# Turning the written key and the normed outputs through DRAM and VectorE's 32x32 blocks in a one-core decoder layer

## The chip, the cores and the metric

The kernel runs on one core of a Trainium2 chip. The metric is the device time of one launch in microseconds (us). The engines are named as in the profile: PE (TensorE), with PEld for its weight loads, DVE (VectorE), ACT (ScalarE), POOL (GpSimd) and SP (SyncE, which here only issues DMAs).

## The reference

One decoder layer over 512 tokens of width 2048, in float32. RWKV time mixing on 16 heads of 64 channels runs beside a multi-scale pooling group, and both are gated and go through one output projection:

```
h = rms_norm(x, norm_g);  z = h @ w_in          # r, k, v, two loras | gate | pool input | pool gate
r, k, v, wd, ad = token_shift_lerp(z)
S_t = S_{t-1} (diag(w_t) - kk_t^T (a_t * kk_t)) + v_t^T k_t ;  y_t = S_t r_t     # per head, 512 steps
y   = head_group_norm(y) * ln_w + ln_b ;  y_rwkv = (y + bonus) * silu(gate)
y_pool = (window means - token) @ w_pool * pool_scale * silu(gate)
x = x + concat(y_rwkv, y_pool) @ w_out
x = x + sigmoid(x @ w_pg + b_pg) * (p @ w_ple) ;  out = rms_norm(x, final_g)
```

## The kernel before, in words

Channels lie on the 128 partitions and tokens along the free dimension. The 16 heads are worked as 8 head pairs j = 0..7 of 128 channels, and the 512 tokens as 8 chunks `ch` of 64. Each float32 projection is three 128x512 matmuls on a high and a low half (`mm3`). A weight chunk of 512 rows x 128 columns is loaded by SP (`raw`, L129), its high half cast by ACT (`whi`, L132), its low half formed by DVE (`wlo`, L133). Each of the three has four buffers, so a load waits for the `wlo` four chunks back, and a cast waits until PE has used the chunk four back; a chunk is 12 matmuls.

PE's program order is written out by hand. `pump(n)` puts n of the large projection matmuls (`zb`, `zg`, `zr`, `zk`, `zv`, ...) between the small ones of the recurrence as filler. A scheduler places the instructions of the other engines when the kernel is built; DVE, ACT and SP then run them strictly in that order. For each pair, `recur(j)` runs the chunks of pair j while pair j+1 is got ready:

- `prepare(j+1)`: the decayed query `ar` and the written key `bk` (two DVE instructions, L596 and L600), and the bonus halves `kph`, `kpl` (L138).
- `scores(j+1)`, after chunk 0: 32 matmuls `pm<-ar,bk`, the masked matrices `mt` (L623), the bonus sum `pbo` and `bv`; four 32-row stores `nd` (L639) and two loads `n` (`n32`, L644) bring blocks of `mt` back in another arrangement. SP issues all of them, in one queue with the weight loads.
- `invert(j+1)`: 31 steps of two small DVE instructions, `tm` (L657) and `xw` (L661), spread over chunks 2 to 7, then `xd` (L665) and `x<-xd` (L672) through DRAM.
- in each chunk: `py` -> `zs` (DVE, L784) -> `pu` -> `uv` (ACT, L794) -> `ps<-uv,bkn` -> `sbd` (DVE, L804 and L806). At ch 3 and ch 7 a visit of 8 small matmul pairs `py<-uv,mt` completes four chunks of outputs, and ACT copies them to `ysb` (L827).
- behind chunk 7: `bn_stats`, `bn_aggr` and a short chain of 128x8 instructions, then eight instructions that normalise `ysb` (L851).
- `gather(j+1)`: TensorE transposes of v (`pv`) and of `bk` (`pbk`, eight of 128x128, copied to `bkn` by ACT, L700); `pending` runs the `finish` of the pair before (`pyt`, four TensorE transposes of `ysb`; ACT L860, DVE L861 and L862, store `yd`). Then two DVE transposes `y<-x` (L723), one for each half of the partitions, whose results `pq` reads with both halves alternating; `scale_key` (the reciprocal of L572); `pq`, `pmv`, `px`. `gather(j)` also computes what pair j+1 needs from k (`prepare_key`, `norm_key`, `scale_key`).

After the last pair come the output projection (`acc_o`, from `yin` read back from `yd`, split into `yhi` and `ylo`) and the embedding gate (`acc_g`).

Of the kernel before, what the change touches and what calls it, by code (L numbers as in the profile page):

```python
# [34 lines left out]
def trunk_kernel(ctx: ExitStack, tc: tile.TileContext, x, p, norm_g, w_in, mu, w0, w_up, a0, a_up,  # L35
# [84 lines left out]
    def dp(o, i):  # L120
        return dprm[:, o + i:o + i + 1]
# [34 lines left out]
    def mm(*a, **k):  # L156
        i = nc.tensor.matmul(*a, **k)  # L157
        return tc.keep_in_program_order(i) if pin[0] else i

    def tr(*a):  # L160
        i = nc.tensor.transpose(*a)
        return tc.keep_in_program_order(i) if pin[0] else i
# [414 lines left out]
    def prepare(j):  # L577
        k_, r_, v_ = need("k", j), need("r", j), need("v", j)
        pw, ipw, tha = pws.pop(j)
        kk = kks.pop(j)  # L580
        if j + 1 < NJ:
            load_ab(j + 1)


        ar = rw.tile([P, NCH // 2, 4, C], F32, name=f"ar{j}", tag="ar", bufs=2)
        bk = rw.tile([P, NCH // 2, 4, C], F32, name=f"bk{j}", tag="bk")
        k4 = kk.rearrange("p (q c t) -> p q c t", c=2, t=C)
        pw4 = pw.rearrange("p (q c) t -> p q c t", c=2)
# [7 lines left out]
        nc.vector.tensor_tensor(bk[:, :, 0::3, :], kp.rearrange("p (q c t) -> p q c t", c=2, t=C), i4, ALU.mult)  # L596
# [3 lines left out]
        nc.vector.tensor_tensor(bk[:, :, 1:3, :], k4, i4, ALU.mult)  # L600
        nc.vector.scalar_tensor_tensor(kp, r_, dp(49, j), kp, ALU.mult, ALU.mult)
        kph = rw.tile([P, T], F32R, name=f"kph{j}", tag="t", bufs=4)
        kpl = rw.tile([P, T], F32R, name=f"kpl{j}", tag="t", bufs=4)
        split(kph, kpl, kp)

        st_[j] = dict(pw=pw, ar=ar, bk=bk, v_=v_, kp=(kph, kpl))

    def scores(j):
        ar, bk, v_ = (st_[j][n_] for n_ in ("ar", "bk", "v_"))
        kph, kpl = st_[j].pop("kp")  # L610

        mt = rw.tile([P, 2, 8, 2, C], F32, name=f"mt{j}", tag="mt", bufs=2)
        pm = [[psM.tile([P, T], F32, name=f"pm{j}_{par}0", tag="m"),
               psY.tile([P, T], F32, name=f"pm{j}_{par}1", tag="y")] for par in range(2)]
        for par in range(2):
            for q in range(4):
                for h in range(2):
                    rows = slice(64 * h, 64 * h + 64)
                    mm(pm[par][h][:, q * P:(q + 1) * P], bk[rows, q, 2 * par:2 * par + 2, :],
                       ar[rows, q, 2 * par:2 * par + 2, :], start=True, stop=True)  # L620
        for par in range(2):
            for h in range(2):
                nc.vector.tensor_tensor(mt[:, par, h::2, :, :],  # L623
                                        pm[par][h].rearrange("p (u a t) -> p u a t", u=4, a=2),
                                        msk[:, par:par + 2, :].unsqueeze(1).to_broadcast([P, 4, 2, C]), ALU.mult)


        ps = psM.tile([P, T], F32, name=f"pbo{j}", tag="m")
        mm(ps, blk, kph, start=True, stop=False)
        mm(ps, blk, kpl, start=False, stop=True)  # L630
        bv = rw.tile([P, T], F32, name=f"bv{j}", tag="bv", bufs=2)
        nc.vector.tensor_tensor(bv, ps, v_, ALU.mult)

        nd = dram.tile([2, 2, 8, 32, 32], F32, name=f"nd{j}", tag="nd")
        for par in range(2):
            pb = 64 * (1 - par)
            for b in range(2):
                rows = slice(pb + 32 * b, pb + 32 * b + 32)
                nc.sync.dma_start(out=nd[par, b].rearrange("u r c -> r u c"),  # L639
                                  in_=mt[rows, par, :, 1 - par, 32 * b:32 * b + 32])  # L640
        nb = []
        for i in range(2):
            t_ = rw.tile([P, 16, 32], F32, name=f"n32{j}_{i}", tag=("kk", "kp")[i])
            nc.sync.dma_start(out=t_, in_=nd[:, :, :, 16 * i:16 * i + 16, :].rearrange(  # L644
                "a b u r c -> (a b u) r c").unsqueeze(0).to_broadcast([4, 32, 16, 32]))
            nb.append(t_)
        st_[j].update(mt=mt, nb=nb, bv=bv)


    def invert(j):  # L650
# [26 lines left out]

    def gather(j):
        d = st_[j]
        bk, v_, mt = d.pop("bk"), d.pop("v_"), d["mt"]  # L680
        if j + 1 < NJ:
            prepare_key(j + 1)
            decay_and_rate(j + 1)
# [7 lines left out]
        nc.scalar.copy(uv[64:128, 1::2, :], pv[64:128])  # L691


        bkn = rw.tile([P, NCH, P], F32, name=f"bkn{j}", tag="bkn")
        for hf in range(2):
            ps = psM.tile([P, T], F32, name=f"pbk{j}_{hf}", tag="m")
            for i in range(4):
                ch = 4 * hf + i
                tr(ps[:, i * P:(i + 1) * P], bk[:, ch // 2, 2 * (ch % 2):2 * (ch % 2) + 2, :], ident)
            nc.scalar.copy(bkn[:, 4 * hf:4 * hf + 4, :], ps.rearrange("p (c n) -> p c n", n=P))  # L700

        pump(H4)

        d.update(uv=uv, bkn=bkn)
        if j + 1 < NJ:
            norm_key(j + 1)
        pump(H5)
        if pending:
            pending.pop()()
        pump(HX)  # L710

        x1 = d["x1"]
# [34 lines left out]
        nc.scalar.copy(zsp[0][64:128, :].rearrange("p (h t) -> p h t", h=2), psv[64:128, 0:2, :])  # L747
        nc.scalar.copy(mv.rearrange("p q (h t) -> p (q h) t", h=2), psv)
        d["mv"] = mv
        pump(2 * H1)  # L750


    def recur(j, work, between):
        d = st_.pop(j)
        pw, ar, mt, bv, uv, bkn, mv, x1 = (d[n_] for n_ in ("pw", "ar", "mt", "bv", "uv", "bkn", "mv", "x1"))
        hop = [0]
        HC1, HC2, HC3 = HC
        lead = [None]
# [8 lines left out]


        ysb = rw.tile([P, NT, P], F32, name=f"ysb{j}", tag="t", bufs=4)
        py = None  # L770
        for ch in range(NCH):
            par, q = ch % 2, ch // 2
            pb = 64 * (1 - par)
# [1 line left out]
            pcc = pw[:, ch, C:C + 1]  # L775
            sl = slice((ch % 4) * P, (ch % 4 + 1) * P)
            if ch % 4 == 0:
                py = psY.tile([P, T], F32, name=f"py{j}_{ch}", tag="y")
            zs = zsp[par]
            if ch > 0:  # L780
                mm(py[:, sl], ar[:, q, 2 * par:2 * par + 2, :], cur, start=ch in (1, 4), stop=True,
# [15 lines left out]
            if ch < NCH - 1:  # L797
# [12 lines left out]
                if ch < NCH - 2:  # L810
                    for h in range(2):
                        hc = slice(64 * h, 64 * h + 64)
                        nc.gpsimd.tensor_scalar(s0p[hc, :], nxt[hc, hc], pcn[hc], None, ALU.mult)  # L813
            if ch % 4 == 3:
                for qq in range(2):
                    for h in range(2):
                        for pr in range(2):
                            c_ = ch - 3 + 2 * qq + pr
                            yr = slice(64 * pr, 64 * pr + 64)
                            o_ = (2 * qq + pr) * P + 64 * h  # L820
                            mm(py[yr, o_:o_ + 64], mt[:, pr, 2 * (c_ // 2) + h, pr, :],
                                             uv[:, c_, 64 * h:64 * h + 64], start=False, stop=True,
                                             skip_group_check=True)
                py4 = py.rearrange("p (s c) -> p s c", c=P)
                for pr in range(2):
                    yr = slice(64 * pr, 64 * pr + 64)
                    nc.scalar.copy(ysb[yr, q - 1:q + 1, :], py4[yr, pr::2, :])  # L827
# [22 lines left out]
        for i in range(8):  # L850
            nc.vector.tensor_scalar(y8[:, i, :], y8[:, i, :], mvr[:, i, 0:1], rs8[:, i, :],  # L851
                                    ALU.subtract, ALU.mult)

        def finish():
            sg = need("g", j)
            ps = psM.tile([P, T], F32, name=f"pyt{j}", tag="m")
# [28 lines left out]
    for j in range(NJ):  # L885
# [292 lines left out]
```

## Time and profile before

| quantity | value |
|---|---|
| time, median of 3 runs | 1094.34 us (1093.44 to 1331.12) |
| profiled execution | 1094.06 us |
| its span, first to last instruction | 1092.3 us |
| granted TensorE clock, mean | 0.998 |
| PE / PEld / DVE / ACT / POOL busy | 1067.4 / 879.1 / 707.9 / 448.2 / 74.4 us |
| DMA packets | 178485, 138.56 MB |

The span is what the trace covers; the profiled execution's own time is 1.8 us more. The head pairs take from about 38 to 711 us, about 75 us each, and the output projection and gate the rest. Busy times are sums; since DVE, ACT and SP run in a fixed order, what an instruction has ahead of it on its engine matters as much as what it reads.

### The profile page before, as it was taken

What the parts mean: (1) busy time and instruction counts of PE and PEld (TensorE: products, weight loads), DVE (VectorE), ACT (ScalarE), POOL (GpSimd) and SP (SyncE); (2) the same over time, 40 slices, a digit from 0 to 9 for tenths busy, and PEclk for the clock granted to TensorE, in tenths of its full rate; (3) what the DMA queues carried; (4) which work ended last, traced back from release to release, by engine and by line L of the source; (5) the groups of instructions that cost most, each with busy time, mean ns of one, the idle gap of its engine ahead of it and who ended that gap; (6) DMA issues with size and microseconds to landing.
All of it is one profiled execution on the core that took longest, in us unless ns stands there. A gap on an engine that the chain in (4) does not pass through costs nothing.

```text
span 1092.3 us, 17194 instructions
## 1 busy us (share of the span) xinstructions
PE 1067.4 (98%) x6060; PEld 879.1 (80%) x6060; DVE 707.9 (65%) x1835; ACT 448.2 (41%) x917; POOL 74.4 (7%) x180
## 2 busy tenths in 40 slices
PE   5999999999999999999999999999999999999996
PEld 4888878888888888787888788888888888888885
DVE  6687867878779679678886956454433424445366
ACT  7633534435335335353443344544222222233337
POOL 2100010110110110100101101000000000000000
PEclk9999999999999999999999999999999999999999
DMA  7433433332423333333334242774534438454534
GB/s 233 116 97 97 112 92 79 102 101 72 127 81 102 105 91 89 95 83 90 94 93 120 79 138 94 231 242 163 171 123 141 164 97 261 129 187 147 174 105 154
DMA packets 178485, 138.56 MB, mean 127 GB/s; under 512 B 34677, under 2 KB 139742, under 8 KB 178398
## 3 DMA queue, kind: packets, MB, share of 16 engines
q1 hardware_dynamic: 157694, 103.89, 32.2%
q10 hardware_dynamic: 20704, 33.56, 9.5%
q8 instruction: 48, 0.79, 0.3%
q14 instruction: 39, 0.32, 0.1%
HBM read 118.02 MB, written 18.87 MB: 125 GB/s over the span
## 4 chain that ended last, share of the span: by engine, by line
PE 88%; DVE 5%; DMA 3%; ACT 2%; issue 1%; SPq 0%; ACTq 0%; DVEq 0%
PE acc_o L157 16%; PE acc_g L157 16%; PE zb L157 15%; PE zv L157 8%; PE zr L157 7%; PE zg L157 7%; PE zk L157 6%; DMA n<-nd 2%; PE py L157 2%; PE pple L157 2%; PE pu L157 2%; PE pm L157 1%; PE pp L157 1%; PE ps L157 1%; PE pmv L157 1%
## 5 line engine op out<-in xcount | busy, mean ns | idle before, releaser
L133 DVE TENSOR_TENSOR wlo_g<-raw_g,whi_g 128x512 fp32r<-128x512 f32 x84 | 56.9, 683 | 78.7 <-ACT whi_g L132 78.5
L157 PE MATMUL zb<-hhi,whi_b 128*128 128x512 f32 x256 | 106.3, 415 | 0.0
L133 DVE TENSOR_TENSOR wlo_o<-raw_o,whi_o 128x512 fp32r<-128x512 f32 x64 | 43.9, 690 | 92.3 <-ACT whi_o L132 92.2
L157 PE MATMUL zb<-hhi,wlo_b 128*128 128x512 f32 x256 | 100.5, 393 | 0.0
L157 PE MATMUL acc_o<-whi_o,ylo 128*128 128x512 f32 x256 | 100.2, 391 | 0.0
L157 PE MATMUL acc_o<-whi_o,yhi 128*128 128x512 f32 x256 | 99.9, 390 | 0.0
L157 PE MATMUL zb<-hlo,whi_b 128*128 128x512 f32 x256 | 99.8, 390 | 0.0
L157 PE MATMUL acc_o<-wlo_o,yhi 128*128 128x512 f32 x256 | 99.7, 389 | 0.0
L132 ACT CAST whi_g<-raw_g 128x512 fp32r<-128x512 f32 x84 | 51.9, 620 | 105.5 <-PE acc_g L157 60.3
L157 PE MATMUL acc_g<-whi_g,x2hi 128*128 128x512 f32 x208 | 81.2, 391 | 0.0
L157 PE MATMUL acc_g<-wlo_g,x2hi 128*128 128x512 f32 x208 | 81.0, 389 | 0.0
L157 PE MATMUL acc_g<-whi_g,x2lo 128*128 128x512 f32 x208 | 80.6, 389 | 0.0
L132 ACT CAST whi_o<-raw_o 128x512 fp32r<-128x512 f32 x64 | 39.9, 623 | 97.8 <-PE acc_o L157 97.8
L813 POOL TENSOR_SCALAR s0p<-sbd,pw 64x64 f32<-64x64 f32 x96 | 56.7, 590 | 338.5 <-DVE sbd L806 253.7
L132 ACT CAST whi_b<-raw_b 128x512 fp32r<-128x512 f32 x64 | 39.7, 620 | 87.1 <-PE zv L157 34.9
L133 DVE TENSOR_TENSOR wlo_b<-raw_b,whi_b 128x512 fp32r<-128x512 f32 x64 | 43.7, 684 | 34.2 <-ACT whi_b L132 33.0
L157 PEld LDWEIGHTS zb<-hhi,wlo_b 128*128 128x128 f32 x256 | 48.0, 188 | 11.0
L661 DVE TENSOR_TENSOR xw<-xw,tm 128x60 f32<-128x60 f32 (+24 forms) x248 | 51.9, 209 | 6.8
L157 PEld LDWEIGHTS acc_o<-wlo_o,yhi 128*128 128x128 f32 x256 | 48.1, 188 | 10.0
L157 PEld LDWEIGHTS acc_o<-whi_o,ylo 128*128 128x128 f32 x256 | 48.1, 188 | 9.9
L157 PEld LDWEIGHTS acc_o<-whi_o,yhi 128*128 128x128 f32 x256 | 48.1, 188 | 9.6
L157 PEld LDWEIGHTS zb<-hhi,whi_b 128*128 128x128 f32 x256 | 48.3, 189 | 8.4
(285 smaller groups left out, 2546.8 us busy)
## 6 DMA issues: line engine op xcount, KB each, us to landing
raw_b<-in_w_in_dram SPq DMA_DIRECT2D x64, 256.0 KB
raw_o<-in_w_out_dram SPq DMA_DIRECT2D x64, 256.0 KB
raw_g<-in_w_pg_dram SPq DMA_DIRECT2D x64, 256.0 KB
raw_k<-in_w_in_dram SPq DMA_DIRECT2D x32, 256.0 KB
raw_r<-in_w_in_dram SPq DMA_DIRECT2D x32, 256.0 KB
raw_v<-in_w_in_dram SPq DMA_DIRECT2D x32, 256.0 KB
raw_g<-in_w_in_dram SPq DMA_DIRECT2D x32, 256.0 KB
n<-nd SPq DMA_DIRECT2D x16, 256.0 KB
```

The source lines that it names most:

```text
L132: nc.scalar.copy(hi, raw)
L133: nc.vector.tensor_tensor(lo, raw, hi.bitcast(F32), ALU.subtract)
L157: i = nc.tensor.matmul(*a, **k)
L661: nc.vector.tensor_tensor(xw[:, 0:n_, s + 1:32], xw[:, 0:n_, s + 1:32], tm[:, 0:n_, 0:w_], ALU.add)
L813: nc.gpsimd.tensor_scalar(s0p[hc, :], nxt[hc, hc], pcn[hc], None, ALU.mult)
```

## The change

The transposes of the written key and of the normed outputs leave TensorE. `bk` is stored to DRAM (`bkd`, SP) as soon as it is made; in `scores` four SP loads bring it back as `bg`, with 32x32 blocks arranged so that DVE's transpose, which turns each 32x32 block in its place, finishes the job: `turn_key` is one 128x512 DVE instruction for each half, `bkn<-bg`. The normalised `ysb` goes the same way: store `yb`, four loads `yg` (`fetch`, in the first half of the old `finish`), one DVE transpose `yo<-yg` and the rest as before (`finish`, moved behind half of the last pump of `gather`). `bg` and `yg` share the buffer tag of `bk` (one buffer). `bkn` becomes one tile for all pairs. The `py<-uv,mt` products of all eight chunks, and the copies to `ysb`, come in one visit at ch 7 instead of two.

```diff
 def prepare(j):
-        st_[j] = dict(pw=pw, ar=ar, bk=bk, v_=v_, kp=(kph, kpl))
+        bkd = dram.tile([P, NCH * P], F32, name=f"bkd{j}", tag="bkd")
+        nc.sync.dma_start(out=bkd, in_=bk.rearrange("p q s c -> p (q s c)"))
+        st_[j] = dict(pw=pw, ar=ar, bk=bk, bkd=bkd, v_=v_, kp=(kph, kpl))
+    bkn = rw.tile([P, NCH, P], F32, name="bkn")
+    def turn_key(j, hf):
+        cs = slice(4 * hf, 4 * hf + 4)
+        nc.vector.transpose(bkn[:, cs, :].rearrange("p c (b k) -> p (c b) k", k=32),
+                            st_[j]["bg"][:, cs, :, :].rearrange("p c b k -> p (c b) k"))
 def scores(j):
+        bg = rw.tile([P, NCH, 4, 32], F32, name=f"bg{j}", tag="bk")
+        for q in range(4):
+            nc.sync.dma_start(out=bg[32 * q:32 * q + 32],
+                              in_=st_[j]["bkd"].rearrange("(b k) (c q i) -> q k c b i", b=4, q=4, i=32)[q])
 def gather(j):
-        bkn = rw.tile([P, NCH, P], F32, name=f"bkn{j}", tag="bkn")
-        for hf in range(2):
-            ps = psM.tile([P, T], F32, name=f"pbk{j}_{hf}", tag="m")
-            for i in range(4):
...
-            nc.scalar.copy(bkn[:, 4 * hf:4 * hf + 4, :], ps.rearrange("p (c n) -> p c n", n=P))
+        if j == 0:
+            turn_key(0, 0)
+            turn_key(0, 1)
         pump(H4)
...
         if pending:
-            pending.pop()()
+            pending[0][0]()
         pump(HX)
...
-        pump(2 * H1)
+        pump(H1)
+        if pending:
+            pending.pop()[1]()
+        pump(H1)
 def recur(j, work, between):
+            if ch in (4, 7) and j + 1 < NJ:
+                with tc.issue_after(lead[0].ins):
+                    turn_key(j + 1, ch // 7)
-            if ch % 4 == 3:
...
+            if ch == NCH - 1:
+                for c0 in range(0, NCH, 4):
...
+        yb = dram.tile([P, T], F32, name=f"yb{j}", tag="yb")
+        nc.sync.dma_start(out=yb, in_=ysb.rearrange("p t c -> p (t c)"))
+        def fetch():
+            yg = rw.tile([P, NCH, 4, 32], F32, name=f"yg{j}", tag="bk")
+            for q in range(4):
+                nc.sync.dma_start(out=yg[32 * q:32 * q + 32, 0:NT],
+                                  in_=yb.rearrange("(b k) (t q i) -> q k t b i", b=4, q=4, i=32)[q])
+            fetched.append(yg)
         def finish():
-            for tt in range(NT):
-                tr(ps[:, tt * P:(tt + 1) * P], ysb[:, tt, :], ident)
...
-            nc.scalar.activation(yo, ps, AF.Identity, scale=dp(57, j), bias=dp(65, j))
+            nc.vector.transpose(yo.rearrange("p (b k) -> p b k", k=32), yg[:, 0:NT].rearrange("p t b k -> p (t b) k"))
+            nc.scalar.activation(yo, yo, AF.Identity, scale=dp(57, j), bias=dp(65, j))
...
-    pump(HE)
-    pending.pop()()
+    pump(HE // 2)
+    pending[0][0]()
+    pump(HE // 2)
+    pending.pop()[1]()
```

The scheduler also arranges the instructions of DVE and SP differently around the new ones. Three places follow; the digit behind a name's stem is the pair or chunk set it belongs to (`bk4` is pair 4's, `wlo_k5_2` is piece 2 of pair 5's k weights), the digits behind the last underscore only number the buffer, and line numbers are those of each kernel's own file.

SP's queue around pair 4's loads `n`, during `recur(3)`, before:

```order
L129 DMA raw_r5_2_2634<-in_w_in_dram 128x4x128
L639 DMA nd4_4661<-mt4_4631 32x8x32 x4
L129 DMA raw_r5_3_2669<-in_w_in_dram 128x4x128
L644 DMA n324_0_4666<-nd4_4661 128x1x512
L644 DMA n324_1_4668<-nd4_4661 128x1x512
L129 DMA raw_v5_0_2675<-in_w_in_dram 128x4x128
L129 DMA raw_v5_1_2732<-in_w_in_dram 128x4x128
```

and with the change:

```order
L607 DMA bkd4_4561<-bk4_4546 128x1024
L648 DMA nd4_4657<-mt4_4627 32x8x32 x2
L658 DMA bg4_4666<-bkd4_4561 32x32x32
L648 DMA nd4_4657<-mt4_4627 32x8x32
L129 DMA raw_r5_3_2667<-in_w_in_dram 128x4x128
L648 DMA nd4_4657<-mt4_4627 32x8x32
L658 DMA bg4_4666<-bkd4_4561 32x32x32
L129 DMA raw_v5_0_2673<-in_w_in_dram 128x4x128
L129 DMA raw_v5_1_2735<-in_w_in_dram 128x4x128
L653 DMA n324_0_4662<-nd4_4657 128x1x512
L653 DMA n324_1_4664<-nd4_4657 128x1x512
```

The two loads `n` have moved behind two weight loads and two of the `bg` loads.

DVE's order ahead of pair 4's `mt`, that is, what runs up to and around PE's `pm` of `scores(4)`, before (`bk4` L596 is seven rows further up):

```order
L600 TENSOR_TENSOR bk4_4552<-kk4_4294,ipw4_4314 128x4x128
L133 TENSOR_TENSOR wlo_k5_0_2461<-raw_k5_0_2458,whi_k5_0_2460 128x512
L601 SCALAR_TENSOR_TENSOR kp4_4553<-sr4_4076,dprm_133,kp4_4553 128x512
L804 TENSOR_SCALAR sbd1_567<-ps3_0_4594,pw3_3343 64x64 x2
L526 TENSOR_TENSOR as5_4550<-ar5_4547,as5_4550 64x128
L138 TENSOR_TENSOR kpl4_4564<-kp4_4553,kph4_4563 128x512
L133 TENSOR_TENSOR wlo_k5_1_2489<-raw_k5_1_2486,whi_k5_1_2488 128x512
L133 TENSOR_TENSOR wlo_k5_2_2495<-raw_k5_2_2492,whi_k5_2_2494 128x512
L623 TENSOR_TENSOR mt4_4631<-pm4_00_4632,msk_108 128x4x128
```

and with the change:

```order
L819 TENSOR_SCALAR sbd1_567<-ps3_0_4590,pw3_3350 64x64 x2
L133 TENSOR_TENSOR wlo_k5_1_2479<-raw_k5_1_2476,whi_k5_1_2478 128x512
L133 TENSOR_TENSOR wlo_k5_2_2485<-raw_k5_2_2482,whi_k5_2_2484 128x512
L883 STREAM_TRANSPOSE yo2_4525<-yg2_4386 128x512
L596 TENSOR_TENSOR bk4_4546<-kp4_4547,ipw4_4320 128x4x2x64
L600 TENSOR_TENSOR bk4_4546<-kk4_4300,ipw4_4320 128x4x128
L885 TENSOR_TENSOR yo2_4525<-yo2_4525,bv2_2719 128x512
L601 SCALAR_TENSOR_TENSOR kp4_4547<-sr4_4069,dprm_133,kp4_4547 128x512
L886 TENSOR_TENSOR yo2_4525<-yo2_4525,sg2_2829 128x512
L138 TENSOR_TENSOR kpl4_4558<-kp4_4547,kph4_4557 128x512
L632 TENSOR_TENSOR mt4_4627<-pm4_00_4628,msk_108 128x4x128
```

Both halves of `bk4` now stand behind `yo2<-yg2`, whose buffer they take over, and behind `wlo_k5_2`.

DVE's order around the two transposes `y<-x` of `gather(1)` (`y11`), before:

```order
L851 TENSOR_SCALAR ysb0_1663<-ysb0_1663,mvr0_2327,rs80_2344 128x64 x5
L133 TENSOR_TENSOR wlo_b1_2_1385<-raw_b1_2_1382,whi_b1_2_1384 128x512
L851 TENSOR_SCALAR ysb0_1663<-ysb0_1663,mvr0_2327,rs80_2344 128x64 x3
L568 TENSOR_SCALAR kk2_2367<-pss2_2438 128x512
L723 STREAM_TRANSPOSE y11_2507<-x11_2258 32x256 x2
L572 RECIPROCAL kk2_2367<-kk2_2367 128x512
```

and with the change:

```order
L568 TENSOR_SCALAR kk2_2375<-pss2_2433 128x512
L150 TENSOR_TENSOR nt80_2353<-nt80_2353,rs80_2350 128x8
L731 STREAM_TRANSPOSE y11_2497<-x11_2253 32x256
L151 SCALAR_TENSOR_TENSOR rs80_2350<-nt80_2353,rs80_2350 128x8
L572 RECIPROCAL kk2_2375<-kk2_2375 128x512
L133 TENSOR_TENSOR wlo_b1_3_1411<-raw_b1_3_1408,whi_b1_3_1410 128x512
L133 TENSOR_TENSOR wlo_g2_0_1417<-raw_g2_0_1414,whi_g2_0_1416 128x512
L867 TENSOR_SCALAR ysb0_1662<-ysb0_1662,mvr0_2333,rs80_2350 128x64 x8
L370 SCALAR_TENSOR_TENSOR sv2_2443<-zv2_2222,prm_131,sv2_2443 128x511
L731 STREAM_TRANSPOSE y11_2497<-x11_2253 32x256
```

The second transpose has moved from just ahead of the reciprocal to behind it and eleven instructions more, the eight that normalise `ysb0` among them. In `gather(0)`, `gather(2)`, `gather(4)` and `gather(5)` the reciprocal stands between the two transposes too; in `gather(3)`, `gather(6)` and `gather(7)` it does not.

More of the change, by code (lines that the diff above doesn't have):

```diff
@@ L646, in scores @@
             nb.append(t_)
-        st_[j].update(mt=mt, nb=nb, bv=bv)
+        bg = rw.tile([P, NCH, 4, 32], F32, name=f"bg{j}", tag="bk")
+        for q in range(4):
+            nc.sync.dma_start(out=bg[32 * q:32 * q + 32],
+                              in_=st_[j]["bkd"].rearrange("(b k) (c q i) -> q k c b i", b=4, q=4, i=32)[q])
+        st_[j].update(mt=mt, nb=nb, bv=bv, bg=bg)
     def invert(j):
@@ L679, in gather @@
         d = st_[j]
-        bk, v_, mt = d.pop("bk"), d.pop("v_"), d["mt"]
+        v_, mt = d.pop("v_"), d["mt"]
         if j + 1 < NJ:
@@ L691, in gather @@
         nc.scalar.copy(uv[64:128, 1::2, :], pv[64:128])
-        bkn = rw.tile([P, NCH, P], F32, name=f"bkn{j}", tag="bkn")
-        for hf in range(2):
-            ps = psM.tile([P, T], F32, name=f"pbk{j}_{hf}", tag="m")
-            for i in range(4):
-                ch = 4 * hf + i
-                tr(ps[:, i * P:(i + 1) * P], bk[:, ch // 2, 2 * (ch % 2):2 * (ch % 2) + 2, :], ident)
-            nc.scalar.copy(bkn[:, 4 * hf:4 * hf + 4, :], ps.rearrange("p (c n) -> p c n", n=P))
+        if j == 0:
+            turn_key(0, 0)
+            turn_key(0, 1)
         pump(H4)
-        d.update(uv=uv, bkn=bkn)
+        d.update(uv=uv)
         if j + 1 < NJ:
@@ L749, in gather @@
         d["mv"] = mv
-        pump(2 * H1)
+        pump(H1)
+        if pending:
+            pending.pop()[1]()
+        pump(H1)
     def recur(j, work, between):
         d = st_.pop(j)
-        pw, ar, mt, bv, uv, bkn, mv, x1 = (d[n_] for n_ in ("pw", "ar", "mt", "bv", "uv", "bkn", "mv", "x1"))
+        pw, ar, mt, bv, uv, mv, x1 = (d[n_] for n_ in ("pw", "ar", "mt", "bv", "uv", "mv", "x1"))
         hop = [0]
@@ L769, in recur @@
         ysb = rw.tile([P, NT, P], F32, name=f"ysb{j}", tag="t", bufs=4)
-        py = None
+        pys = {}
         for ch in range(NCH):
@@ L777, in recur @@
             if ch % 4 == 0:
-                py = psY.tile([P, T], F32, name=f"py{j}_{ch}", tag="y")
+                pys[ch // 4] = psY.tile([P, T], F32, name=f"py{j}_{ch}", tag="y")
+            py = pys[ch // 4]
             zs = zsp[par]
@@ L813, in recur @@
                         nc.gpsimd.tensor_scalar(s0p[hc, :], nxt[hc, hc], pcn[hc], None, ALU.mult)
-            if ch % 4 == 3:
[L815 to L827, printed above, removed]
+            if ch == NCH - 1:
+                for c0 in range(0, NCH, 4):
+                    py = pys[c0 // 4]
+                    for qq in range(2):
+                        for h in range(2):
+                            for pr in range(2):
+                                c_ = c0 + 2 * qq + pr
+                                yr = slice(64 * pr, 64 * pr + 64)
+                                o_ = (2 * qq + pr) * P + 64 * h
+                                mm(py[yr, o_:o_ + 64], mt[:, pr, 2 * (c_ // 2) + h, pr, :],
+                                   uv[:, c_, 64 * h:64 * h + 64], start=False, stop=True, skip_group_check=True)
+                    py4 = py.rearrange("p (s c) -> p s c", c=P)
+                    for pr in range(2):
+                        yr = slice(64 * pr, 64 * pr + 64)
+                        nc.scalar.copy(ysb[yr, c0 // 2:c0 // 2 + 2, :], py4[yr, pr::2, :])
             step()
@@ L852, in recur @@
                                     ALU.subtract, ALU.mult)
+        yb = dram.tile([P, T], F32, name=f"yb{j}", tag="yb")
[6 more added lines that the diff above has]
+            fetched.append(yg)
         def finish():
-            sg = need("g", j)
-            ps = psM.tile([P, T], F32, name=f"pyt{j}", tag="m")
-            for tt in range(NT):
-                tr(ps[:, tt * P:(tt + 1) * P], ysb[:, tt, :], ident)
+            sg, yg = need("g", j), fetched.pop()
             yo = rw.tile([P, T], F32, name=f"yo{j}", tag="t", bufs=4)
-            nc.scalar.activation(yo, ps, AF.Identity, scale=dp(57, j), bias=dp(65, j))
+            nc.vector.transpose(yo.rearrange("p (b k) -> p b k", k=32), yg[:, 0:NT].rearrange("p t b k -> p (t b) k"))
+            nc.scalar.activation(yo, yo, AF.Identity, scale=dp(57, j), bias=dp(65, j))
             nc.vector.tensor_tensor(yo, yo, bv, ALU.add)
@@ L863, in finish @@
             nc.scalar.dma_start(out=yd[j], in_=yo)
-        pending.append(finish)
+        pending.append((fetch, finish))
     HC, HT, HX = (6, 9, 9), 130, 13
@@ L869, in trunk_kernel @@
     HP = 1000
-    pending = []
+    pending, fetched = [], []
     need("k", 0)
```

## The prediction

> **What bounds the kernel now.** I read the page first: the busy shares and the chain that ended last. Then the busy times by stretch, to see whether the share holds stage by stage and which clock was granted there, and last the timeline around the places that the change touches.
>
> ```profile
> PE 1067.4 (98%) x6060; PEld 879.1 (80%) x6060; DVE 707.9 (65%) x1835; ACT 448.2 (41%) x917; POOL 74.4 (7%) x180
> PE 88%; DVE 5%; DMA 3%; ACT 2%; issue 1%; SPq 0%; ACTq 0%; DVEq 0%
> 340.00:415.00 75.00, 74.80 (x488) 61.44 (x488) 58.62 (x175) 31.42 (x69) 8.27 (x15) 1.00 0.36 102
> ```
>
> PE is busy for 98% of the span, and the chain lies on PE for 88%. The stretch from 340 to 415 us, about one head pair, says it more sharply (length, then each engine's busy time, granted clock, DMA share, GB/s): PE 74.80 of 75 us at clock 1.00, DVE 58.62, DMA engines at 0.36. So the filler matmuls hide nearly every wait of the recurrence. Two things follow. Work taken off PE comes off the time one for one. And since PE's order is fixed, it has no reserve: every new wait of a small matmul adds its full length, because the filler behind it may not overtake it. The change must be judged by what PE saves against what PE newly waits for.
>
> **What is removed.**
>
> ```profile
> 329.90 0.40 PE L157 MATMUL zv<-hhi,wlo_v 128*128 128x512 f32 x1
> 330.22 0.69 PE L157 MATMUL py<-uv,mt 128*64 128x64 f32 x16
> 330.84 0.50 PE L157 MATMUL zb<-hhi,whi_b 128*128 128x512 f32 x1
> 331.17 0.40 PE L157 MATMUL zb<-hlo,whi_b 128*128 128x512 f32 x1
> 334.38 1.04 PE L161 MATMUL pbk<-ident,bk 128*128 128x128 f32 x8
> 335.17 0.47 PE L157 MATMUL zb<-hhi,whi_b 128*128 128x512 f32 x1
> 340.50 0.69 PE L161 MATMUL pyt<-ident,ysb 128*128 128x128 f32 x4
> 340.94 0.48 PE L157 MATMUL zb<-hhi,whi_b 128*128 128x512 f32 x1
> ```
>
> Columns: start, duration, engine, line, operation. From one start to the next, the eight `pbk` take 0.79 us, and the four `pyt` 0.44: about 0.11 us each with their change-over. Per pair 12 go, 96 in all: 10.6 us. The two ACT copies of `pbk` cost nothing now (ACT is at 41%). A `py` visit takes 0.62 us; merging two keeps all the products and saves one change-over per pair, which must be bounded: nothing, or up to 0.36 if some of the 0.62 goes too. The filler ahead of the visit reaches to the next start in 0.32 us and the one behind it in 0.33, where fillers otherwise follow at 0.23 us; those 0.2 us, eight times, are nearest: 1.5. **Gain: 12.1 us**, which alone gives 1094.06 - 12.1 = 1082.
>
> **What is added to DVE.**
>
> ```profile
> L723 DVE STREAM_TRANSPOSE y<-x 32x256 f32<-32x256 f32 x16 | 6.9, 430 | 1.2 <-DMA x<-xd 1.0
> L133 DVE TENSOR_TENSOR wlo_g<-raw_g,whi_g 128x512 fp32r<-128x512 f32 x84 | 56.9, 683 | 78.7 <-ACT whi_g L132 78.5
> ```
>
> A 128x512 transpose isn't in this trace. Bounds: 0.43 us (a quarter of the partitions, half the columns, so it can't be less) and, were it twice the 256 columns' time, 0.86; a plain 128x512 instruction takes 0.68. I take 0.70. Three per pair make 2.1 us, inside the 16 us per pair that DVE idles. By count DVE can carry it; the cost is where the order puts it.
>
> **Wait 1: the second `y<-x` behind the reciprocal (`pq`).** In `gather(1)`:
>
> ```profile
> 181.15 0.69 PE L157 MATMUL py<-uv,mt 128*64 128x64 f32 x16
> 187.94 1.20 DVE L851 TENSOR_SCALAR ysb<-ysb,mvr,rs 128x64 f32<-128x64 f32 x5
> 190.93 0.89 DVE L723 STREAM_TRANSPOSE y<-x 32x256 f32<-32x256 f32 x2
> 191.86 3.35 DVE L572 RECIPROCAL kk<-kk 128x512 f32<-128x512 f32 x1
> 195.13 0.63 DVE L133 TENSOR_TENSOR wlo_b<-raw_b,whi_b 128x512 fp32r<-128x512 f32 x1
> 195.40 0.69 PE L157 MATMUL pq<-y,mt 32*32 32x32 f32 x32
> ```
>
> Before, both transposes are done at 191.82, 3.6 us ahead of `pq`. After, the reciprocal starts at 191.86 + 0.6 (the visit is twice as long) + 0.6 (`kp` L592 now ahead) - 1.9 (eight `ysb` instructions of 0.22 to 0.24, now behind) - 0.46 (second transpose) = 190.7. Behind it come 3.3, two `wlo` at 0.6 (the spacing of 128x512 instructions back to back, as the four `mt` in 2.48 us below), `ysb` 1.8, `sv` 0.7 and the transpose's 0.45: 198.2. PE asks at 195.40 + 0.6 - 1.2 (12 transposes fewer) = 194.8. Stall about 3.5. The same sum along the rows of the other swapped gathers gives 0.9 (2), 5.2 (4) and 3.6 (5); in 3, 6 and 7 both transposes precede the reciprocal: nothing. `gather(0)` is the worst, because its inversion starts late as well:
>
> ```profile
> 82.67 1.22 SPq L644 DMA_DIRECT2D n<-nd  x2
> 86.16 0.62 ACT L132 CAST whi_r<-raw_r 128x512 fp32r<-128x512 f32 x1 [1.60 <-issue]
> 89.14 0.19 DVE L657 TENSOR_TENSOR tm<-i,n 128x31 f32<-128x31 f32 x1 [3.75 <-DMA n<-nd]
> 116.83 0.89 DVE L723 STREAM_TRANSPOSE y<-x 32x256 f32<-32x256 f32 x2
> 120.90 0.69 PE L157 MATMUL pq<-y,mt 32*32 32x32 f32 x32
> ```
>
> Its `n` loads now stand behind pair 1's first v piece, which takes the buffer of a `wlo` whose cast ran at 86.16: issue near 88 instead of 82.67, so the steps start 5.5 us later, and two `bkn` transposes plus two more `wlo` fall inside the steps: x1 is about 8.4 us late, 125.2. With the reciprocal between, the second transpose ends at 128.9 and PE asks at 120.0: 8.9. **Sum 22.1.**
>
> **Wait 2: `pm` behind `bk`.** In `scores(4)`:
>
> ```profile
> 348.66 0.68 DVE L596 TENSOR_TENSOR bk<-kp,ipw 128x512 f32<-128x512 f32 x1
> 352.99 0.68 DVE L600 TENSOR_TENSOR bk<-kk,ipw 128x512 f32<-128x512 f32 x1
> 355.69 0.68 DVE L138 TENSOR_TENSOR kpl<-kp,kph 128x512 fp32r<-128x512 f32 x1
> 357.76 0.62 ACT L132 CAST whi_k<-raw_k 128x512 fp32r<-128x512 f32 x1 [1.65 <-PE zg L157]
> 357.83 2.06 PE L157 MATMUL pm<-ar,bk 64*128 64x128 f32 x32
> 358.41 0.69 DVE L133 TENSOR_TENSOR wlo_k<-raw_k,whi_k 128x512 fp32r<-128x512 f32 x1 [1.44 <-ACT whi_k L132]
> 359.13 2.48 DVE L623 TENSOR_TENSOR mt<-pm,msk 128x512 f32<-128x512 f32 x4
> ```
>
> Before, `bk` was ready 4 us ahead of `pm`. After, both halves stand behind the `wlo_k` of 358.41, whose cast PE itself releases just as it reaches `pm`, and behind `yo<-yg`. So, from 357.83: 0.6 to that `wlo`, 0.6 for it, 0.7 for `yo`, 0.6 and 0.69 for `bk`, 0.1 to start: 3.3 us, whenever PE arrives. The bounds are 2.5 (transpose at 0.43, less overlap) and whatever a late `yg` adds. By each pair's own rows 2 to 7 give 2.6, 3.4, 3.3, 1.0, 3.1 and 2.5. **Sum 15.9.** Then `kpl`, once 2.1 us ahead of `pm`, comes behind `bk`, two `yo` and `kp`: 361.1 + 2.5 = 363.6 against 363.4 for the second `pbo`; 0.2 to 1.75 by pair, **5.0 together**.
>
> **Wait 3: the loads `n` in SP's queue (`zs`).**
>
> ```profile
> 365.09 1.15 SPq L644 DMA_DIRECT2D n<-nd  x2
> 367.73 3.45 SPq L129 DMA_DIRECT2D raw_v<-in_w_in_dram  x2
> 372.85 0.19 DVE L657 TENSOR_TENSOR tm<-i,n 128x31 f32<-128x31 f32 x1 [2.08 <-DMA n<-nd]
> 376.89 0.28 DVE L784 TENSOR_TENSOR zs<-py,mv 64x128 f32<-64x128 f32 x1
> DVE tm L657 <- DMA n<-nd: 18.3, 8, 3.8
> ```
>
> The last row (from the waits: sum, times, longest) says that in every pair DVE already stands still for `n`. With the change `n` is issued behind the second `raw_v`, which goes out near 370.8 (the end of its row, 371.18, less one issue of 0.4): 371.3 instead of 365.09, usable 6.5 to 7.8 us later (the two pairs of rows shown), near 378. Behind this first `tm` nine steps precede the `zs` of chunk 3, 2.0 us: `zs` near 380 instead of 376.89, and `py`, `pu` and their `ps` hang on it. Less what was waited before, I get 2.6 for pair 4, and 11.7 over pairs 1 to 7 (one of them gains 1.5). It could shrink to nothing where waits 1 and 2 have already held PE back.
>
> **Wait 4: the tail.**
>
> ```profile
> 727.28 0.39 PE L157 MATMUL acc_o<-whi_o,ylo 128*128 128x512 f32 x1
> 727.36 0.61 ACT L132 CAST whi_o<-raw_o 128x512 fp32r<-128x512 f32 x1
> 728.10 0.69 DVE L133 TENSOR_TENSOR wlo_o<-raw_o,whi_o 128x512 fp32r<-128x512 f32 x1
> ```
>
> The first `ylo` (done long before 727.28) now stands behind this `wlo_o` and a `sgp`: 728.7 + 0.7 + 0.7, or 2.8 us late.
>
> **The sum.** 22.1 + 15.9 + 5.0 + 11.7 + 2.8 = 57.5 of waits, less 12.1, is +45.4, or 1139.5 against the profiled 1094.06 (0.3 us below the median). Some of wait 3 will lie under the others; I set 4 us off for it and forecast **1135 us**.
>
> A rule that speaks against the change: the Trainium skill, "VectorE: DVE Perf Modes", in its three transpose paths, says that VectorE turns 32x32 blocks only, and its rules for authors advise TensorE for a 128x128 transpose if PSUM may take the result. The rows agree: 0.11 us each on PE. By that rule the sum cannot end below 1094, where PE's rows alone give 1082; it is why the case in which only the saving shows has a small chance below.
>
> **The rivals.**
>
> *The waits are hidden and only the saving shows: 1082.* One mechanism: DVE idles 16 us in a stretch of 75, and if it enters each gather and each `scores` some 4 us earlier than I assume, it stands ahead of PE at all four places. For it speaks that idle time; against it, that the cast of wait 2 is released by PE itself. It decides at 3.3 us per place. It is also what remains if the change does only what it says. Chance 0.10, with 0.03 below 1072.5.
>
> *Half the waits: 1098 to 1120.* Only waits 1 and 2 come (22.1 + 15.9 - 12.1 = +26, or 1120), or only one of them (+4 to +10). For it: a PE that has been held up at `pq` leaves DVE and SP time to catch up before `pm` and `zs`; against it: the cast of wait 2. Chance 0.22.
>
> *The small packets starve the queues: about 1165.*
>
> ```profile
> q1 hardware_dynamic: 157694, 103.89, 32.2%
> ```
>
> The `bg` and `yg` loads move runs of 128 bytes: 32 x 1024 + 32 x 512 = 49,152 more packets. 32.2% of 16 x 1092.3 us over 157,694 is 35.7 ns per packet; at that price 110 us of all engines, 13.7 per pair, raising 0.36 to 0.54. That fits, unless a load goes over few engines and the weights queued behind come late: at 3 to 4 us per pair, +25 on the forecast. Chance 0.13. The Trainium skill, "DMA: Bandwidth & Descriptors", in its specifications, says that transfers under 512 bytes fall short of line rate because they read, modify and write; no run here shows that yet.
>
> **How the numbers follow.** The forecast (1120 to 1150) has 0.55. A measurement of this kernel tells 2%, 22 us, from no change: below 1072.5 is faster, above 1116.2 slower. Faster 0.03; within 2% 0.17 (0.07 of the hidden case, 0.10 of the half); slower 0.80. The range of eight in ten leaves out the hidden case and half of the starved one: 1098 to 1162.
>
> **What would show it.** `pq` starts 3 to 9 us late behind a DVE transpose in gathers 0, 1, 4 and 5; `pm` waits 2.5 to 3.4 us for `bk` L600; the wait of `tm` for `n` exceeds 18.3 us; DVE transposes of 0.7. PE busy falls by about 10 us while its share falls to 93%. I am wrong if `pm` starts beside the cast of the last `whi_k`, if `n` is issued less than 7 us after `pm`, or if `raw` loads hold the casts.

## The result, and the profile after

The changed kernel takes 1178.98 us (median of 5 runs, 1175.25 to 1180.11) against 1094.34: a ratio of 1.0768, 95% interval 1.0749 to 1.0788. That is 84.6 us slower. The direction was forecast, the size was not: 1135 us, range 1098 to 1162. The profiled execution has a span of 1177.3 us, 85.0 more than before. The 1331.12 us in the range of the kernel before is a slow execution and is not in the ratio.

The page of the changed kernel: busy shares, granted clock in 40 slices, and the chain that ended last.

```profile
PE 1085.7 (92%) x5964; PEld 892.8 (76%) x5964; DVE 722.0 (61%) x1859; ACT 442.1 (38%) x901; POOL 69.4 (6%) x180
PEclk9999799899999898998999999998999999999999
PE 78%; DVE 11%; DMA 6%; issue 2%; ACT 2%; SPq 0%; ACTq 0%; DVEq 0%
```

PE runs 96 instructions fewer, as it should, and yet is busy 18.3 us longer (1067.4 before). The slices of the clock, all at 9 before, now dip: the mean granted clock of the run is 0.963 against 0.998. In the chain, DVE's share rises from 5% to 11% and DMA's from 3% to 6%.

What PE waited for, from the waits (engine, line, releaser: total us, times, longest); the last row is a wait of DVE. Before the change PE waited 1.7 us at `pu` and not at all at `pm`, `pq` and `acc_o`, and DVE's `tm` 18.3 us:

```profile
PE pu L157 <- DVE zs L796: 18.9, 10, 3.9
PE pm L157 <- DVE bk L600: 17.6, 5, 4.0
PE pq L157 <- DVE y L731: 17.0, 4, 6.4
PE acc_o L157 <- DMA yin<-yd: 9.8, 1, 9.8
PE pq L157 <- DVE sw L420: 4.9, 1, 4.9
DVE tm L670 <- DMA n<-nd: 29.6, 8, 5.4
```

(The last `pq` row is the same kind of wait; the releaser named is a neighbour of the second `y<-x`.) Adding up every stretch of over 0.12 us in which PE had nothing running, up to its last matmul, gives 82.3 us, against 15.6 before: **66.7 us of new waits**. With 18.3 us of additional busy time that is the whole 85.0.

The timeline of `gather(1)`, to be laid beside the one shown of before:

```profile
202.15 0.44 DVE L731 STREAM_TRANSPOSE y<-x 32x256 f32<-32x256 f32 x1
202.71 3.35 DVE L572 RECIPROCAL kk<-kk 128x512 f32<-128x512 f32 x1
207.11 1.87 DVE L867 TENSOR_SCALAR ysb<-ysb,mvr,rs 128x64 f32<-128x64 f32 x8
209.56 0.42 DVE L731 STREAM_TRANSPOSE y<-x 32x256 f32<-32x256 f32 x1
206.11 0.24 PE L157 MATMUL pq<-y,mt 32*32 32x32 f32 x2
210.03 1.05 PE L157 MATMUL pq<-y,mt 32*32 32x32 f32 x30 [3.68 <-DVE y L731]
211.01 1.97 PE L157 MATMUL pmv<-uv,mt 64*64 64x64 f32 x32
214.50 0.63 PE L157 MATMUL zb<-hlo,whi_b 128*128 128x512 f32 x1
```

The wait itself is as predicted: 3.68 us for 3.5. But look at what follows: `pmv` took 1.15 us before and takes 1.97, and the filler `zb` 0.63 instead of 0.39. The busy times by stretch (length, each engine, granted clock, DMA share, GB/s) around the same place give the reason:

```profile
204.00:210.00 6.00, 2.36 (x12) 1.62 (x10) 6.00 (x14) 0.58 (x1) 0.00 (x0) 1.00 0.33 96
210.00:216.80 6.80, 6.77 (x101) 5.94 (x102) 3.71 (x7) 2.91 (x7) 0.40 (x1) 0.51 0.23 57
216.80:224.00 7.20, 7.20 (x35) 6.00 (x34) 2.55 (x6) 2.24 (x5) 0.89 (x2) 0.99 0.39 97
```

For 6.8 us after the wait PE is granted half its clock (0.51). The trace's clock record has fourteen such stretches before the last matmul, each at 0.5, each a multiple of 3.41 us long, each beginning 2 to 5 us after a wait of PE began, and none elsewhere; before the change there is none until PE has finished. PE worked for 67.1 us inside them. If all of it took twice as long, that cost 33.6 us. The fillers behind the row shown start 0.43 us apart, against 0.23 at full clock; at that price it is an estimated 67.1 x (1 - 0.23/0.43) = **31 us**. With 18.3 us of additional busy time, the removed work then saved 13 us, 15.3 at most (12.1 predicted).

### The profile page after: what moved, and what is told of

Same layout as the page of the kernel before. It is cut to its first block, busy times and chain, and to the rows that moved or that the text cites. A ratio compares the mean times of both kernels' runs of the same rounds, so it can differ in the third digit from the quotient of the medians.

```text
span 1177.3 us, 17118 instructions
## 1 busy us (share of the span) xinstructions
PE 1085.7 (92%) x5964; PEld 892.8 (76%) x5964; DVE 722.0 (61%) x1859; ACT 442.1 (38%) x901; POOL 69.4 (6%) x180
## 3 DMA queue, kind: packets, MB, share of 16 engines
q1 hardware_dynamic: 210174, 116.48, 34.7%
## 4 chain that ended last, share of the span: by engine, by line
PE 78%; DVE 11%; DMA 6%; issue 2%; ACT 2%; SPq 0%; ACTq 0%; DVEq 0%
PE acc_o L157 15%; PE acc_g L157 15%; PE zb L157 12%; PE zv L157 7%; PE zr L157 6%; PE zg L157 6%; PE zk L157 5%; DMA n<-nd 3%; PE pple L157 2%; PE pm L157 2%; PE pu L157 1%; PE py L157 1%; DVE tm L670 1%; DVE kk L572 1%; DVE xw L674 1%
## 5 line engine op out<-in xcount | busy, mean ns | idle before, releaser
L828 POOL TENSOR_SCALAR s0p<-sbd,pw 64x64 f32<-64x64 f32 x96 | 52.8, 550 | 393.6 <-DVE sbd L821 306.9
L157 PEld LDWEIGHTS acc_o<-whi_o,yhi 128*128 128x128 f32 x256 | 48.8, 190 | 19.9 <-issue 10.1
L157 PEld LDWEIGHTS acc_o<-wlo_o,yhi 128*128 128x128 f32 x256 | 48.6, 190 | 10.2
```

## The experiments

All times stand against the kernel before, run on the same chip. Three theories: (A) the waits are where the order puts them, and each long one also brings half-clock work behind it; (B) the waits are right but the clock fell for another reason; (C) the 49,152 small packets and the longer queues slow everything. In the tables the columns on PE and the clock are of the one execution that was profiled, the times are medians.

**One edge for each wait, and all three.** `e1` chains the second `y<-x` to the first:

```diff
-            for pb in (0, 64):
-                yt = nc.vector.transpose(y1[pb:pb + 32], x1[pb:pb + 32, :, 0:32])
+            yt = nc.vector.transpose(y1[0:32], x1[0:32, :, 0:32])
+        with tc.issue_after(yt.ins):
+            yt = nc.vector.transpose(y1[64:96], x1[64:96, :, 0:32])
```

`e2` gives `yg` other buffers, `e3` issues `bg` after `n`:

```diff
-            yg = rw.tile([P, NCH, 4, 32], F32, name=f"yg{j}", tag="bk")
+            yg = rw.tile([P, NT, 4, 32], F32, name=f"yg{j}", tag="t", bufs=4)
...
+        with tc.issue_after(nld.ins):
             for q in range(4):
                 nc.sync.dma_start(out=bg[32 * q:32 * q + 32],
```

> The changed kernel with one ordering edge more: the second transpose y<-x is issued after the first, so that both stand ahead of the reciprocal again in all gathers; nothing else differs. Theory A (waits plus clock: each new wait costs its own length, and the half-clock stretch behind it as much again of PE's work): in the changed kernel pq waits 22.5 us and PE works 30.4 us at half clock right behind these waits, worth 15.2 us, so 1179 - 38 = about 1141 us. Theory B (waits alone, the clock's fall has another cause): 1179 - 22 = about 1157 us, granted clock still near 0.963. Theory C (the small packets and longer queues slow everything): within 5 us of 1179.

> The changed kernel with yg taken from the buffers of tag t (four of 2 KB) in place of bk's single buffer, so bk no longer has to wait for yo<-yg. Theory A: the waits of pm (17.6 us) and pbo (1.3) go, and 9.2 us of half clock with them: about 1151 us. Theory B: 1179 - 19 = 1160 us. Theory C: within 5 us of 1179.

> The changed kernel with the four bg loads of each pair issued after the pair's two loads n in SP's queue, so n goes out earlier. Theory A: the waits of pu for zs (19.1 us, of which 1.8 were there before the change) go and 6.6 us of half clock: about 1155 us. Theory B: 1162 us. Theory C: within 5 us of 1179.

> All three edits together; the transposes still go through DRAM and VectorE, all small packets are still moved. Theory A: only the tail's wait (9.8 us and 2.6 of clock) stays, and PE's saving shows: 1094 - 12 + 12 = about 1094 us, granted clock near 0.99. Theory B: 1179 - 59 = about 1120, or the clock stays low. Theory C: above 1160 us.

| kernel | median us | ratio to before, interval | PE without work, us | PE at half clock, us | clock |
|---|---|---|---|---|---|
| changed | 1178.98 | 1.0768 [1.0749, 1.0788] | 82.3 | 67.1 | 0.963 |
| e1: `y<-x` in order | 1158.48 | 1.0588 [1.0558, 1.0617] | 69.4 | 48.7 | 0.971 |
| e2: `yg` elsewhere | 1151.25 | 1.0521 [1.0501, 1.0541] | 62.9 | 55.8 | 0.968 |
| e3: `n` before `bg` | 1144.22 | 1.0455 [1.0439, 1.0470] | 54.9 | 51.8 | 0.971 |
| e4: all three | 1108.27 | 1.0111 [1.0086, 1.0135] | 36.5 | 20.8 | 0.985 |

Three small edits of order and buffers take back 70.7 of 84.6 us, with every transpose and every packet still in place; theory C, which gave less than 5 us for each, falls. `e2` met A's number, in part by luck: the 17.6 us at `pm` went as expected and the waits of `pu` fell by 11.3 us besides, but `pbo` (6.6) and `py` (5.8) came in their place. `e1` missed A's number (1141 expected) and landed on B's 1157, but not for B's reason: of the wait in `gather(0)`, 6.36 us before the first transpose and 3.30 before the second, only the second part went and 6.2 us stayed, and waits of 1.57 and 2.23 us at `pq` were left, each still with 6.83 us of half clock. `e3` did better than expected (1155): the wait in `gather(0)` vanished whole. `n` came early there, and in that gather the built order also has both transposes ahead of the reciprocal, so `e3` does not separate the two. `e4` missed A's 1094 by 14 us. What it still waits for:

```profile
PE acc_o L157 <- DMA yin<-yd: 9.1, 1, 9.1
PE pbo L157 <- DVE kpl L138: 7.5, 3, 2.9
PE pq L157 <- DVE y L733: 3.8, 2, 2.2
```

The first row is the tail, as expected. The `pbo` row (0.8 us in the changed kernel) is the price of the second edit: `kpl` shares tag `t` with `yg` there and stands behind the transpose. These rows and 20.8 us at half clock are what keeps `e4` from 1094.

**Is it the wait that halves the clock?** `e5` leaves every transfer, transpose and matmul of the kernel before alone and only holds DVE up ahead of `y<-x`:

```diff
+            with tc.issue_after(late[0].ins):
+                for w_ in PROBE[j]:
+                    for _ in range(2):
+                        late[0] = nc.vector.reciprocal(kk_[:, 0:w_], kk_[:, 0:w_])
```

> The kernel before, with DVE held up by extra reciprocals (taken twice, so the value stays nearly the same) ahead of the two transposes y<-x in gathers 1 to 6: 4.3, 4.6, 4.4, 6.0, 7.8 and 9.1 us of them. No transfer, no order of SP, no transpose is changed. pq should wait about 0.7, 1.9, 2.7, 3.5, 4.2 and 5.8 us: 18.8 in all. Theory A (a wait of PE by itself brings the half clock behind it): the waits up to 2 us cost their length alone; behind the four longer ones stand half-clock stretches of 3.4 to 10 us, together 20 to 30 us of PE's work, 10 to 15 us more: 1123 to 1128 us. Theory B (the clock's fall has another cause, the transfers or the transposes): granted clock stays 0.998 and the time is about 1113 us.

Measured: 1151.77 us, ratio 1.0522 [1.0492, 1.0552]. From its page, waits and stretches (around `gather(4)`):

```profile
PE 1087.7 (94%) x6060; PEld 896.0 (78%) x6060; DVE 743.9 (65%) x1851; ACT 448.4 (39%) x917; POOL 72.1 (6%) x180
q1 hardware_dynamic: 157694, 103.89, 30.4%
PE pq L157 <- DVE y L729: 39.5, 6, 9.6
440.00:446.30 6.30, 4.34 (x21) 3.23 (x20) 6.30 (x8) 2.52 (x5) 0.00 (x0) 1.00 0.19 54
446.30:452.00 5.70, 0.00 (x0) 0.00 (x0) 5.64 (x11) 0.00 (x0) 0.00 (x0) 0.51 0.44 136
452.00:460.00 8.00, 7.89 (x105) 6.81 (x106) 7.16 (x7) 2.92 (x7) 0.54 (x1) 0.50 0.01 2
460.00:468.00 8.00, 8.00 (x45) 6.46 (x44) 4.67 (x9) 3.48 (x7) 1.98 (x2) 1.00 0.27 76
```

The delays came out larger than I meant (39.5 us of waits for 18.8), since other instructions slipped in between the reciprocals; the absolute forecast missed for that. The question is answered all the same. For waits of 39.5 us, B would have given about 1134 us (1094.3 + 39.5). PE runs the same 6060 instructions, with the same 157,694 packets in queue q1, and is busy 20.3 us longer; 47.2 us of its work lies in six stretches at half clock, one at each of the six waits. B falls: a wait alone does it, and here 39.5 us of waiting cost 59.2 us of span. The estimate by the fillers' spacing gives 47.2 x (1 - 0.23/0.43) = 22 us for the 20.3.

**The parts by themselves.**

> The kernel before with the key's part of the change alone: bkd, bg, turn_key, no pbk; visits and outputs as before. In the built order n still stands behind raw_v, and in gather 0 the reciprocal stands between the two transposes, elsewhere not; bk does not wait for yo. Theory A: minus 7.0 us for 64 transposes, plus the waits for zs and in gather 0 (17 + 9.7) and their half clock (6.6 + 4.4): about 1125 us. Theory C (the packets themselves): 32,768 of the 49,152 small packets stay, so two thirds of the loss, about 1150 us.

> The kernel before with the py<-uv,mt products of all chunks in one visit at ch 7, nothing else. By the prediction's term: eight change-overs of 0.2 us fewer, 1092.8 us (0 to 2.9 less). A rival: normalisation and pyt come later by the longer visit and the tail or the DVE order pays it back: 1094 to 1100.

> The kernel before with the outputs' part alone: yb, yg, the DVE transpose, the later finish, no pyt; key and two visits as before. Theory A: 3.5 us saved; at the tail acc_o waits about 10 us and 2.6 us of half clock follow; the first half of bk stands behind yo<-yg but two wlo earlier than in the change, so pm waits 0 to 1 us a pair: 1103 to 1110 us. Theory C: 16,384 small packets, a third of the loss: about 1122.

The key alone: 1119.79 us, 1.0214 [1.0190, 1.0237]; waits of `pu` 15.8 and of `pq` 9.5 us, near what A had (17 and 9.7, 1125 us in all). The outputs alone: 1108.48, 1.0127 [1.0114, 1.0140], within A's 1103 to 1110, with 11.8 us at the tail. The visits alone were the surprise: 1115.08 us, 1.0173 [1.0151, 1.0196], where I expected a small gain. From its waits and timeline:

```profile
PE pyt L161 <- DVE ysb L853: 14.0, 8, 5.3
348.88 3.35 DVE L572 RECIPROCAL kk<-kk 128x512 f32<-128x512 f32 x1
353.42 1.87 DVE L853 TENSOR_SCALAR ysb<-ysb,mvr,rs 128x64 f32<-128x64 f32 x8
354.09 1.73 PE L161 MATMUL pyt<-ident,ysb 128*128 128x128 f32 x4 [5.27 <-DVE ysb L853]
```

With all products at ch 7, all statistics come there too, the eight instructions that normalise `ysb` slip behind the 3.35 us reciprocal, and PE's transposes `pyt`, still at their old place, wait 14.0 us and bring 14.5 us of work at half clock. In the whole change there is no `pyt` to wait, and `finish` moved later with it; `e10` below tests that move.

**Putting it in order.**

> The kernel before with the key's part and the merged visits, both transposes y<-x kept ahead of the reciprocal, the bg loads issued after n; outputs turned on PE as before. Theory A: 7.0 and 1.5 us saved and no new wait: about 1086 us. Theory C: the small packets of bg cost something by themselves: above 1094.

> The kernel before with the key's part alone, both transposes y<-x ahead of the reciprocal, the bg loads issued after n; two visits and pyt as before. The single visit cost 20 us by making pyt wait, so without it theory A gives only the saving: 1094.3 - 7.0 = about 1087 us, granted clock 0.99 or more. Theory C (the small packets of bg cost something by themselves): 1094 or above.

> As the run with key and merged visits in good order, but finish with its TensorE transposes pyt moved behind the first half of gather's last pump, as in the change. Theory A: pyt no longer waits for the normalised outputs; 7.0 us saved, and 1.5 for the merged visits: about 1086 us. If it stays above 1100, the single visit costs somewhere else too.

> The three edits together (both transposes ahead of the reciprocal, yg from tag t, bg after n), and the last pair's outputs turned on TensorE as before, so that the output projection does not wait for the round trip through DRAM. Theory A: the tail's 9.1 us and about 2 us of half clock go: 1108 - 11 = 1097 us. If the tail's wait stays, it did not come from the round trip.

`e10` takes `e8` and moves the finish, TensorE transposes and all; `e12` takes `e4` and lets the last pair keep the old finish:

```diff
-        if pending:
-            pending.pop()()
         pump(HX)
...
-        pump(2 * H1)
+        pump(H1)
+        if pending:
+            pending.pop()()
+        pump(H1)
```

| kernel | median us | ratio to before, interval | PE without work, us | PE at half clock, us |
|---|---|---|---|---|
| e8: key, one visit, ordered | 1117.68 | 1.0206 [1.0186, 1.0226] | 36.0 | 19.2 |
| e9: key, two visits, ordered | 1099.00 | 1.0036 [1.0024, 1.0048] | 21.2 | 6.8 |
| e10: e8 with `pyt` later | 1092.26 | 0.9975 [0.9961, 0.9988] | 20.1 | 6.8 |
| e12: e4, last pair on PE | 1098.39 | 1.0026 [1.0008, 1.0044] | 26.8 | 6.8 |

`e8` (1086 expected) missed by the `pyt` wait just seen (19.9 us); `e10`, which only moves the finish, takes 25 us off it. `e12` (1097 expected) confirms the tail: the 9.1 us at `acc_o` are gone. `e9` and `e10` were expected at 1087 and 1086 and missed by 12 and 6 us. One wait of 2 to 3 us at `pq` in `gather(5)` and half clock behind it remain in both, and in `e10` another of 2.0 us at `pm`. In `e9` PE is without work 5.6 us longer than before, and its 6.8 us at half clock cost an estimated 3, which is 9 of the 12. By its number alone `e9` falls on C's side (1094 or above); `e10`, with the same packets, falls on the other.

`e12` also shows the clock without any edit: over its twelve executions the time rises from 1092.35 us at a granted clock of 0.996 to 1101.48 at 0.988. The difference in clock, 0.008 of 1098 us, is 8.8 us, and that of the times 9.1. Its profiled execution (1094.75 us) is one of the quicker ones, so 6.8 us at half clock is less than usual for it.

The page of `e10`:

```profile
PE 1060.0 (97%) x5996; PEld 874.0 (80%) x5996; DVE 715.0 (66%) x1851; ACT 441.2 (40%) x901; POOL 70.8 (6%) x180
PEclk9999999999999999999999999999999999999999
q1 hardware_dynamic: 192126, 112.28, 36.2%
```

It is the one version that beats the kernel before, by 0.1 to 0.4%. That is the key's transposes off TensorE, the merged visits and the later finish together; no run has the last two without the first, so the gain can't be divided. The key alone, in order (`e9`), is 0.4% slower than before.

## Why the prediction was wrong, point by point

- **The reading of the bound held.** PE's fixed order has no reserve, and each new wait but that of the tail came out where the order of the instructions had put it.
- **The failed step is "every new wait of a small matmul adds its full length".** It adds more: the length, and up to half of PE's work in a stretch of 3.4 to 13.7 us that then runs at half clock. I had read the clock (1.00 throughout) as a fact about the chip; it was a fact about a PE that hardly paused. The trace already held the warning that I left out: between 38 and 711 us PE has not one gap of over 1.1 us. This term, absent from the sum, is 31 to 34 us, most of the 39.6 that are missing between +45.4 and +85.0; the waits themselves came to 66.7 us for 57.5.
- **Wait 1 (`pq`)**: 22.1 predicted, 22.5 measured, gather by gather 8.9, 3.5, 0.9, 5.2, 3.6 against 9.7, 3.7, 0.7, 4.9, 3.7. This was worked from the order and the spacing of rows alone, and it held.
- **Wait 2 (`pm`, `pbo`)**: 15.9 and 5.0 predicted, 17.6 and 1.3 measured. In `scores(4)` the place is as drawn, but a late `yg` adds its 0.75 us, the upper end that I had named:

```profile
388.98 0.69 DVE L133 TENSOR_TENSOR wlo_k<-raw_k,whi_k 128x512 fp32r<-128x512 f32 x1 [2.03 <-ACT whi_k L132]
390.43 0.71 DVE L883 STREAM_TRANSPOSE yo<-yg 128x512 f32<-128x512 f32 x1 [0.75 <-DMA yg<-yb]
391.78 0.69 DVE L600 TENSOR_TENSOR bk<-kk,ipw 128x512 f32<-128x512 f32 x1
392.52 3.79 PE L157 MATMUL pm<-ar,bk 64*128 64x128 f32 x32 [4.05 <-DVE bk L600]
```

- **Wait 3 (`zs`)**: 11.7 predicted, of which I set 4 off; 18.9 - 1.7 = 17.2 measured. The place is right, the size is not: the 4 us did not hide, and `n` went out later than I had it. For pair 4 it is issued 15.9 us after `pm` starts (392.52), where the prediction's rows gave 10.2 (361.1 to 371.3); why was not followed. `tm` waited 29.6 us for `n` instead of 18.3.

```profile
408.46 1.20 SPq L653 DMA_DIRECT2D n<-nd  x2
415.21 0.19 DVE L670 TENSOR_TENSOR tm<-i,n 128x31 f32<-128x31 f32 x1 [3.50 <-DMA n<-nd]
```

- **Wait 4 (the tail)**: 2.8 predicted, 9.8 measured. I compared `ylo` with its new neighbours and did not follow the last pair's outputs through DRAM:

```profile
783.70 0.34 SPq L871 DMA_DIRECT2D yb<-ysb  x1
792.79 0.57 SPq L876 DMA_DIRECT2D yg<-yb  x1
796.80 0.71 DVE L883 STREAM_TRANSPOSE yo<-yg 128x512 f32<-128x512 f32 x1 [0.32 <-DMA raw_o<-in_w_out_dram]
804.04 1.78 ACTq L941 DMA_DIRECT2D yin<-yd  x4
809.11 0.76 PE L157 MATMUL acc_o<-whi_o,yhi 128*128 128x512 f32 x1 [9.76 <-DMA yin<-yd]
```

  From the store to the transpose is 13.1 us, where `pyt` took 0.6 on PE. Before, the outputs came in time and `acc_o` did not wait; here PE has run out of filler.
- **The transpose**: 0.70 us assumed, 0.702 and 0.709 measured:

```profile
L614 DVE STREAM_TRANSPOSE bkn<-bg 128x512 f32<-128x512 f32 x16 | 11.2, 702 | 0.0
L883 DVE STREAM_TRANSPOSE yo<-yg 128x512 f32<-128x512 f32 x8 | 5.7, 709 | 4.1 <-DMA yg<-yb 3.8 <-DMA raw_o<-in_w_out_dram 0.3
```

- **The saving**: 12.1 predicted, 13 to 15.3 by the account above; in `e12`, with 92 transposes fewer, PE is busy 10.5 us less, and about 13.7 when the cost of its 6.8 us at half clock is taken off. Ends of matmuls are modelled, so 2 us of this are not resolved. The term for the visits (1.5) had the wrong sign as long as `pyt` stays where it was.
- **The starving rival** stood nearest in number (1165) and can be dropped: `e12` moves 50,224 more packets than the kernel before, nearly all of the change's, at 1.0026 of the time:

```profile
q1 hardware_dynamic: 207918, 115.96, 37.3%
```

  In the changed kernel 52,480 more packets (210,174 against 157,694) took 34.7% of 16 x 1177.3 less 32.2% of 16 x 1092.3, some 17 ns of one engine each, and no wait of PE is put down to a weight load. The Trainium skill, "DMA: Bandwidth & Descriptors", in its specifications, has transfers under 512 bytes below line rate. No run here measures that rate by itself.

The Trainium skill, "TensorE: Matmul & The Clock Gate", in "What's actually happening" and "HAM oscillation", says that the array runs at half rate after about one idle window of 3.4 us and at full rate after a busy one, and its rule is to leave no gaps over some 3.4 us. The half and the multiples of 3.41 us agree. The threshold does not, and the measurement decides: a wait of 1.57 us was followed by half clock in `e1` and not in `e12` (1.55), waits of 2.1 to 2.9 us went either way, and from 3.0 us on it always came.

## What to carry to other kernels

In a kernel like this one, where PE is busy throughout at full clock, price a new wait of 2 to 4 us at its length plus 1.5 to 3 us (up to half of a stretch of 3.41 or 6.83 us), a longer one at more (in `e5`, 59.2 us for 39.5), and look for the clock row before saying that a wait costs what it lasts. Work moved off the bound engine onto an idle one is paid for by where its instructions land in that engine's and the queues' fixed order: follow who stands behind it (a buffer that is taken over, a load that slips behind others, a reciprocal in between) before counting its busy time. And when one part of a change looks like a small gain, ask what its results were early for: the merged visits alone made the kernel 20 us slower, and moving their reader took 25 us off `e8`.

## What was not expected of the hardware

- The granted clock halves after a wait of PE and stays halved in steps of 3.41 us: 3.41 or 6.83 where a wait of 1.6 to 4.1 us brings it, 6.83 to 13.65 after longer ones (6.83 after 8.91 us in `e1`, 13.65 after 7.77 us in `e5`).
- Which of the short waits bring it hangs on where they fall. In every trace with more than one such stretch, all of them begin a whole number of 3.413 us steps apart. Divide each of the 13 traces with half clock into these steps from 20 us on: of the steps at full clock, all 68 in which PE had nothing running for 1.84 us or more were followed by half clock, none of the 3939 with less than 1.28 us was, and 7 of the 29 in between were. A wait that lies inside one step counts whole, one that a step's end divides counts in two parts. What decides between 1.28 and 1.84 us is not settled.
- DVE's transpose of 128x512 takes the time of a plain 128x512 instruction (0.70 against 0.68 us), though one of 32x256 takes 0.43.
